# A mixture of experts: weight loads with a cast inside the DMA, against plain loads by one queue with the cast on VectorE

## The chip, the cores and the metric

The kernel runs on one core of a Trainium2 chip. The metric is the device time of one execution in microseconds (us); lower is better. The time before is 182.22 us, the median of three runs (182.13 to 182.71). The profiled execution spans 180.0 us from its first to its last instruction.

Engines are called PE (TensorE, matrix products), DVE (VectorE), ACT (ScalarE), POOL (GpSimd) and SP (SyncE). The last does no arithmetic here; it only issues transfers. All transfers, whoever issues them, run on the 16 DMA engines of the core.

## The reference

Eight experts, each with 256 tokens of 512 features, a first matrix 512 x 2048 and a second 2048 x 512. Everything is fp32 in memory.

```python
n_experts, capacity, hidden, expert_hidden = 8, 256, 512, 2048
# x [8, 256, 512]  w1 [8, 512, 2048]  w2 [8, 2048, 512]  b1 [8, 2048]  b2 [8, 512]
h = np.matmul(x, w1) + b1[:, np.newaxis, :]
h = np.maximum(h, 0)
return (np.matmul(h, w2) + b2[:, np.newaxis, :]).astype(np.float32)
```

Each w1[e] and each w2[e] has 4.194 MB in fp32, sixteen matrices in all; x and the result have 4.194 MB each.

## The kernel before

The products run in fp16. Every weight matrix is read by a transfer that GpSimd issues and that turns fp32 into fp16 on the way: the tile it writes is fp16. Three buffers hold w1, three hold w2. The last w2 has tiles of its own and comes in three pieces. x of the first two experts is loaded plain by SyncE and cast by VectorE, the rest by GpSimd with a cast.

```python
    LAG = 3
    w1_pool = ctx.enter_context(tc.tile_pool(name="w1", bufs=3))
    w2_pool = ctx.enter_context(tc.tile_pool(name="w2", bufs=3))
    w2t_pool = ctx.enter_context(tc.tile_pool(name="w2t", bufs=1))
    # ...
    def load_w1(e):
        w1_sb[e] = w1_pool.tile([P, nKC, M], fp16, tag="w1", name="w1sb")
        ordered(nc.gpsimd.dma_start(
            out=w1_sb[e], in_=w1[e].rearrange("(p kc) m -> p kc m", kc=nKC)
        ))
    # ... load_w2 and load_w2_piece alike
```

The first product needs x with its features in the partitions. VectorE makes this transposed xT from fp16 x in blocks of 32 x 32, in the middle of the first product of the expert before. The first product has 16 groups of four matmuls; ScalarE takes each group out of PSUM, adds b1 and applies the maximum with 0, and writes hT in fp16.

```python
                    nc.vector.transpose(out=out[:, tb, g], in_=block[:, tb])
    # ...
    def first_product(e):
        hT[e] = hT_pool.tile([P, nJ, T], fp16, tag="hT", name="hT")
        for j in range(nJ):
            bias_at = j * B + e * nB + nB - 1
            ph = psum_h.tile([P, T], fp32, tag="ph", name="ph")
            for kc in range(nKC):
                ordered(nc.tensor.matmul(
                    out=ph,
                    lhsT=w1_sb[e][:, kc, :].rearrange("p (q j) -> p q j", j=nJ)[:, :, j],
                    rhs=xT[e][:, kc, :],
                    start=(kc == 0),
                    stop=(kc == nKC - 1),
                ))
            nc.scalar.activation(
                out=hT[e][:, j, :],
                in_=ph,
                func=mybir.ActivationFunctionType.Relu,
                bias=b1T[:, bias_at : bias_at + 1],
                scale=1.0,
            )
            if j == nJ // 2 and e + 1 < E:
                transposes(e + 1)
```

The second product of expert e comes three steps after its first product (LAG), so four hT are held. It starts with the bias b2 as a matmul of one row and then runs 32 matmuls into two PSUM tiles, which VectorE and ScalarE copy to SBUF, one each. The stores of the first six experts are issued by GpSimd in the same queue as the loads, late, and the last two by SyncE and ScalarE.

```python
    for s in range(E + LAG):
        while ring and ring[0][0] <= s:      # loads and late stores, in a set order
            _, put, args = ring.pop(0)
            put(*args)
        if s < E:
            first_product(s)
        if s >= LAG:
            second_product(s - LAG)
```

Of the kernel before, what the change touches and what calls it, by code (L numbers as in the profile page):

```python
# [7 lines left out]


@with_exitstack  # L10
def kernel(
# [9 lines left out]
    nc = tc.nc  # L21
    fp32 = mybir.dt.float32
    fp16 = mybir.dt.float16
    E, T, H = x.shape
    M = w1.shape[2]
    P = 128
    nTB = T // P
    nKC = H // P
    nJ = M // P
    B = 32  # L30
    nB = P // B
    LAG = 3

    REUSED = {E - 2: 2, E - 1: 3}
    LATE = range(E - 2)


    PARTS = {E - 2: ((0, 25, False), (25, 121, True), (121, 128, False))}  # L40
    nXF32 = 2
    X_LOADS = {2: 2, 4: 4}

    def ordered(ins):
        return tc.keep_in_program_order(ins)

    singles = ctx.enter_context(tc.tile_pool(name="singles", bufs=1))
    w1_pool = ctx.enter_context(tc.tile_pool(name="w1", bufs=3))
    w2_pool = ctx.enter_context(tc.tile_pool(name="w2", bufs=3))
    w2t_pool = ctx.enter_context(tc.tile_pool(name="w2t", bufs=1))  # L50
    x_pool = ctx.enter_context(tc.tile_pool(name="xp", bufs=1))
    xT_pool = ctx.enter_context(tc.tile_pool(name="xTp", bufs=2))
    hT_pool = ctx.enter_context(tc.tile_pool(name="hT", bufs=LAG + 1))
    out_pool = ctx.enter_context(tc.tile_pool(name="outp", bufs=E - 2))
    psum_h = ctx.enter_context(tc.tile_pool(name="psum_h", bufs=3, space=bass.MemoryType.PSUM))
    psum_o = ctx.enter_context(tc.tile_pool(name="psum_o", bufs=2, space=bass.MemoryType.PSUM))

    ones1 = singles.tile([1, P], fp16)
    b2_sb = singles.tile([1, E * H], fp16)
    b1_rows = singles.tile([E * nB, M // nB], fp32)  # L60
    b1T = singles.tile([P, nJ * B + nB - 1], fp32)

    x16 = [None] * E
    xT = [None] * E
    w1_sb = [None] * E
    w2_sb = [None] * E
    hT = [None] * E
    results = []
    pending = {}

    def load_x(first, n):

        R = n * T // P
        t = x_pool.tile([P, R, H], fp16, tag=f"x{first}", name=f"x{first}")
        ordered(nc.gpsimd.dma_start(  # L75
            out=t, in_=x[first : first + n].rearrange("e (p r) h -> (e p) r h", r=R)
        ))
        for i in range(n):
            x16[first + i] = (t, i * (P // n), R)

    def load_w1(e):
        w1_sb[e] = w1_pool.tile([P, nKC, M], fp16, tag="w1", name="w1sb")
        ordered(nc.gpsimd.dma_start(  # L83
            out=w1_sb[e], in_=w1[e].rearrange("(p kc) m -> p kc m", kc=nKC)
        ))

    def load_w2(e):
        src = w2[e].rearrange("(p j) h -> p j h", j=nJ)
        w2_sb[e] = []
        t = w2_pool.tile([P, nJ, H], fp16, tag="w2", name="w2sb")  # L90
        ordered(nc.gpsimd.dma_start(out=t, in_=src))  # L91
        w2_sb[e].append((0, nJ, t))

    def load_w2_piece(e, lo, hi):
        t = w2t_pool.tile([P, hi - lo, H], fp16, tag=f"w2_{lo}", name=f"w2_{lo}")
        src = w2[e].rearrange("(p j) h -> p j h", j=nJ)
        ordered(nc.gpsimd.dma_start(out=t, in_=src[:, lo:hi, :]))  # L97
        if w2_sb[e] is None:
            w2_sb[e] = []
        w2_sb[e].append((lo, hi, t))  # L100

    def transposes(e):


        t, p0, R = x16[e]
        n = R // nTB
        xT[e] = xT_pool.tile([P, nKC, T], fp16, tag="xT", name="xT")
        for g in range(T // R // B):
            src = t[p0 + B * g : p0 + B * (g + 1)]
            for b in range(nB):  # L110
                block = src[:, :, b * (H // nB) : (b + 1) * (H // nB)].rearrange(
                    "p (n tb) (i kc) -> p tb kc n i", tb=nTB, kc=nKC)
                out = xT[e][b * B : (b + 1) * B].rearrange(
                    "p kc (tb g i n) -> p tb g kc n i", tb=nTB, i=B, n=n)
                if n == 1:
                    nc.vector.transpose(out=out[:, :, g, :, 0, :], in_=block[:, :, :, 0, :])  # L116
                    continue
                for tb in range(nTB):
                    nc.vector.transpose(out=out[:, tb, g], in_=block[:, tb])  # L119

    def first_product(e):
        hT[e] = hT_pool.tile([P, nJ, T], fp16, tag="hT", name="hT")
        for j in range(nJ):
            bias_at = j * B + e * nB + nB - 1
            ph = psum_h.tile([P, T], fp32, tag="ph", name="ph")
            for kc in range(nKC):
                ordered(nc.tensor.matmul(  # L127
                    out=ph,
                    lhsT=w1_sb[e][:, kc, :].rearrange("p (q j) -> p q j", j=nJ)[:, :, j],
                    rhs=xT[e][:, kc, :],  # L130
                    start=(kc == 0),
                    stop=(kc == nKC - 1),
                ))
            nc.scalar.activation(  # L134
                out=hT[e][:, j, :],
                in_=ph,
                func=mybir.ActivationFunctionType.Relu,
                bias=b1T[:, bias_at : bias_at + 1],
                scale=1.0,
            )  # L140
            if j == nJ // 2 and e + 1 < E:
                transposes(e + 1)

    def flush(e):
        dst, src = pending.pop(e)
        ordered(nc.gpsimd.dma_start(out=dst, in_=src))  # L146

    def store(e, po):
        if e in REUSED:
            out_sb = results[REUSED[e]]  # L150
        else:
            results.append(out_pool.tile([P, nTB, H], fp32, tag="out", name="out"))
            out_sb = results[e]
        nc.vector.tensor_copy(out=out_sb[:, 0, :], in_=po[0])  # L154
        nc.scalar.copy(out=out_sb[:, 1, :], in_=po[1])  # L155
        dst = out[e].rearrange("(p tb) h -> p tb h", tb=nTB)
        if e in LATE:
            pending[e] = (dst, out_sb)
            return
        for p0, p1, scalar in PARTS.get(e, ((0, P, False),)):  # L160
            (nc.scalar if scalar else nc.sync).dma_start(out=dst[p0:p1], in_=out_sb[p0:p1])

    def second_product(e):
        po = []
        for tb in range(nTB):
            t = psum_o.tile([P, H], fp32, tag=f"po{tb}", name=f"po{tb}")
            po.append(t)
            ordered(nc.tensor.matmul(  # L168
                out=t, lhsT=ones1, rhs=b2_sb[0:1, e * H : (e + 1) * H], start=True, stop=False,
            ))  # L170
        for lo, hi, t in w2_sb[e]:
            for tb in range(nTB):
                for j in range(lo, hi):
                    ordered(nc.tensor.matmul(  # L174
                        out=po[tb],
                        lhsT=hT[e][:, j, tb * P : (tb + 1) * P],
                        rhs=t[:, j - lo, :],
                        start=False,
                        stop=(j == nJ - 1),
                    ))  # L180
        store(e, po)

    x32 = []
    for e in range(nXF32):
        x32.append(out_pool.tile([P, nTB, H], fp32, tag="out", name="x32"))
        nc.sync.dma_start(out=x32[e], in_=x[e].rearrange("(p tb) h -> p tb h", tb=nTB))
    load_w1(0)
    ordered(nc.gpsimd.dma_start(  # L188
        out=b2_sb,
        in_=b2.rearrange("e h -> (e h)").rearrange("(o f) -> o f", o=1),  # L190
    ))
    ordered(nc.gpsimd.dma_start(out=b1_rows, in_=b1.rearrange("e (b i) -> (e b) i", b=nB)))  # L192
    nc.vector.memset(ones1, 1.0)  # L193

    for e in range(nXF32):
        t = x_pool.tile([P, nTB, H], fp16, tag=f"x{e}", name=f"x{e}")
        nc.vector.tensor_copy(out=t, in_=x32[e])  # L197
        x16[e] = (t, 0, nTB)
        if e == 0:
            transposes(e)  # L200


    for b in range(nB):
        nc.vector.transpose(  # L204
            out=b1T[b * B : (b + 1) * B, nB - 1 - b : nB - 1 - b + nJ * B],
            in_=b1_rows.rearrange("r (i j) -> r j i", j=nJ),
        )

    ring = []
    for s in range(1, E + LAG - 1):
        if s < E:
            if s in X_LOADS:
                ring.append((s - 2, load_x, (s, X_LOADS[s])))
            ring.append((s - 2, load_w1, (s,)))
        if s >= LAG:
            ring.append((s - 2, load_w2, (s - LAG,)))
    for lo, hi in ((0, 8), (8, 12), (12, 16)):
        ring.append((0, load_w2_piece, (E - 1, lo, hi)))  # L220
    for e in LATE:
        ring.append((e + LAG + 1, flush, (e,)))

    for s in range(E + LAG):
        while ring and ring[0][0] <= s:
            _, put, args = ring.pop(0)
            put(*args)
        if s < E:
            first_product(s)
        if s >= LAG:  # L230
            second_product(s - LAG)
    assert not ring and not pending


# [28 lines left out]
```

## Time and profile before

| | before |
|---|---|
| time, median of three runs | 182.22 us |
| span of the profile | 180.0 us |
| PE busy (matmuls) | 129.6 us, 72% |
| VectorE busy | 78.0 us, 43% |
| ScalarE busy | 62.2 us, 35% |
| read from HBM, written to HBM | 71.39 MB, 4.19 MB |
| bytes moved as written at the destination | 40.56 MB |
| longest waits on PE for w1 | 23.8 us in 6 waits, the longest 15.1 (the first) |

The profile counts a DMA by what it writes. A load that casts writes half of what it reads, so its GB/s in the slices must be doubled to be compared with a plain load's or a store's. The span is cut into 40 slices of 4.5 us; a digit is the busy share of an engine in tenths. A wait is put down to what ended it. A busy matmul is pipelined with its neighbours, so that the start of one to the start of the next is what it costs, not its own duration. A number in brackets such as (x35) counts the instructions in a stretch.

### The profile page before, as it was taken

How to read it: one execution, taken by the hardware profiler on the slowest of the kernel's cores; microseconds unless marked ns; L12 is line 12 of the kernel's file. 1: busy time of each engine (PE TensorE's matmuls, PEld its weight loads, DVE VectorE, ACT ScalarE, POOL GpSimd, SP SyncE). 2: the span in 40 equal slices, each digit the busy share in tenths (PEclk: the TensorE clock that was granted, in tenths of full speed). 3: DMA queues.
4: the chain of work that ended last, by engine and by line, in shares of the span. 5: the costliest groups of instructions: out<-in, count | busy, mean ns of one | idle time of the engine just before them, and what ended most of it. 6: DMA issues, size and time to landing. Idle time of an engine off the chain costs nothing.

```text
span 180.0 us, 1941 instructions
## 1 busy us (share of the span) xinstructions
PE 129.6 (72%) x784; PEld 86.2 (48%) x784; DVE 78.0 (43%) x111; ACT 62.2 (35%) x137; POOL 15.4 (9%) x32
## 2 busy tenths in 40 slices
PE   0006199969595960999979597959496977999960
PEld 0004179969592420795378245934195422434420
DVE  1999933986000199999980992001000100100030
ACT  0000559969592010483059003930196010010020
POOL 7000002020201010001010001000510101011000
PEclk9999999999998798589999889999999996999996
DMA  6998998999999999999999999999999999999996
GB/s 220 246 233 191 233 226 182 233 228 211 206 233 197 218 226 226 208 208 233 218 200 222 226 218 197 233 218 200 222 226 222 193 233 218 198 217 192 331 420 251
DMA packets 4404, 40.56 MB, mean 225 GB/s; under 512 B 524, under 2 KB 540, under 8 KB 2220
## 3 DMA queue, kind: packets, MB, share of 16 engines
q0 software_dynamic: 3808, 38.35, 96.6%
q1 hardware_dynamic: 476, 1.70, 2.5%
q10 hardware_dynamic: 112, 0.39, 0.6%
q8 instruction: 6, 0.10, 0.2%
q14 instruction: 2, 0.02, 0.0%
HBM read 71.39 MB, written 4.19 MB: 420 GB/s over the span
## 4 chain that ended last, share of the span: by engine, by line
DMA 80%; PE 13%; POOL 2%; issue 1%; another core or an unknown queue 1%; DVE 0%; POOLq 0%; DVEq 0%
DMA w1sb<-in_w_dram 44%; DMA w2sb<-in_w_dram 22%; DMA out_dram<-out 14%; PE ph L127 8%; PE po L174 5%; POOL w1sb L83 1%; DVE out L154 0%; PE po L168 0%; POOL b_rows L192 0%; POOL b_sb L188 0%; POOL x L75 0%; DVEq L154 0%; POOLq L146 0%; POOLq L247 0%
## 5 line engine op out<-in xcount | busy, mean ns | idle before, releaser
L127 PE MATMUL ph<-xT,w1sb 128*128 128x256 f16 x512 | 63.9, 290 | 33.9 <-DMA w1sb<-in_w_dram 23.8
L127 PEld LDWEIGHTS <-w1sb 128*128 128x128 f16 x512 | 59.2, 147 | 39.4 <-DMA w1sb<-in_w_dram 32.3
L119 DVE STREAM_TRANSPOSE xT<-x 32x256 f16<-32x256 f16 (+1 forms) x64 | 52.8, 886 | 30.3 <-DMA x<-in_x_dram 18.7
L134 ACT ACTIVATE hT<-ph,b1T 128x256 f16<-128x256 f32 x128 | 56.3, 474 | 20.2 <-PE ph L127 20.2
L174 PE MATMUL po<-w2sb,hT 128*128 128x512 f16 x224 | 54.5, 406 | 10.3 <-DMA w2sb<-in_w_dram 10.3
L174 PEld LDWEIGHTS <-hT 128*128 128x128 f16 x256 | 26.1, 103 | 45.7 <-issue 20.4
L154 DVE COPY out<-po 128x512 f32<-128x512 f32 x8 | 5.5, 692 | 62.5 <-PE po L174 44.1
L155 ACT COPY out<-po 128x512 f32<-128x512 f32 x8 | 4.7, 585 | 72.6 <-PE po L174 57.5
L116 DVE STREAM_TRANSPOSE xT<-x 32x256 f16<-32x256 f16 x32 | 14.0, 436 | 0.5
L83 POOL DMA_DIRECT2D w1sb<-in_w_dram x8 | 4.7, 591 | 63.0 <-PE ph L127 62.1
L91 POOL DMA_DIRECT2D w2sb<-in_w_dram x7 | 3.7, 534 | 54.5 <-PE po L174 54.5
L134 ACT ACT_TABLE_LOAD x1 | 1.3, 1283 | 20.1 <-DVE b1T L204 20.1
L174 PE MATMUL po<-w,hT 128*128 128x512 f16 x32 | 7.1, 379 | 0.0
L146 POOL DMA_DIRECT2D out_dram<-out x6 | 3.2, 539 | 32.0 <-DMA w2sb<-in_w_dram 27.5
L168 PE MATMUL po<-b_sb,ones 1*128 1x512 f16 x16 | 4.8, 379 | 0.0
L204 DVE STREAM_TRANSPOSE b1T<-b_rows 32x512 f32<-32x512 f32 x4 | 4.1, 1037 | 0.1
L197 DVE CAST x<-x 128x1024 f16<-128x1024 f32 x2 | 1.4, 694 | 3.0 <-DMA x<-in_x_dram 3.0
L168 PEld LDWEIGHTS <-ones 1*128 1x128 f16 x16 | 0.9, 92 | 2.1 <-issue 2.1
L97 POOL DMA_DIRECT2D w<-in_w_dram x3 | 1.6, 546 | 0.0
L75 POOL DMA_DIRECT2D x<-in_x_dram x2 | 1.1, 558 | 0.0
L192 POOL DMA_DIRECT2D b_rows<-in_b_dram x1 | 0.5, 525 | 0.0
L193 DVE MEMSET ones<- 1x128 f16 x1 | 0.2, 165 | 0.8 <-PEq L247 0.8
(5 smaller groups left out, 0.9 us busy)
## 6 DMA issues: line engine op xcount, KB each, us to landing
w1sb<-in_w_dram POOLq DMA_DIRECT2D x8, 2048.0 KB, 34.5
w2sb<-in_w_dram POOLq DMA_DIRECT2D x7, 2048.0 KB, 43.7
out_dram<-out POOLq DMA_DIRECT2D x6, 512.0 KB, 28.6
x<-in_x_dram SPq DMA_DIRECT2D x2, 512.0 KB, 3.6
x<-in_x_dram POOLq DMA_DIRECT2D x1, 1024.0 KB, 30.7
w<-in_w_dram POOLq DMA_DIRECT2D x1, 1024.0 KB, 35.7
w<-in_w_dram POOLq DMA_DIRECT2D x2, 512.0 KB, 38.8
x<-in_x_dram POOLq DMA_DIRECT2D x1, 512.0 KB, 24.1
```

What stands on the lines that cost most here:

```text
L83: ordered(nc.gpsimd.dma_start(out=w1_sb[e], in_=w1[e].rearrange("(p kc) m -> p kc m", kc=nKC)))
L91: ordered(nc.gpsimd.dma_start(out=t, in_=src))
L116: nc.vector.transpose(out=out[:, :, g, :, 0, :], in_=block[:, :, :, 0, :])
L119: nc.vector.transpose(out=out[:, tb, g], in_=block[:, tb])
L127: ordered(nc.tensor.matmul(out=ph, lhsT=w1_sb[e][:, kc, :].rearrange("p (q j) -> p q j", j=nJ)[:, :, j], rhs=xT[e][:, kc, :], start=(kc == 0),
L134: nc.scalar.activation(out=hT[e][:, j, :], in_=ph, func=mybir.ActivationFunctionType.Relu, bias=b1T[:, bias_at : bias_at + 1], scale=1.0,)
L146: ordered(nc.gpsimd.dma_start(out=dst, in_=src))
L154: nc.vector.tensor_copy(out=out_sb[:, 0, :], in_=po[0])
L155: nc.scalar.copy(out=out_sb[:, 1, :], in_=po[1])
L168: ordered(nc.tensor.matmul(out=t, lhsT=ones1, rhs=b2_sb[0:1, e * H : (e + 1) * H], start=True, stop=False,))
L174: ordered(nc.tensor.matmul(out=po[tb], lhsT=hT[e][:, j, tb * P : (tb + 1) * P], rhs=t[:, j - lo, :], start=False, stop=(j == nJ - 1),))
L204: nc.vector.transpose(out=b1T[b * B : (b + 1) * B, nB - 1 - b : nB - 1 - b + nJ * B], in_=b1_rows.rearrange("r (i j) -> r j i", j=nJ),)
```

## The change

The weights are no longer cast in the DMA. SyncE issues all large loads, plain fp32, in one queue and in the order in which they are needed, into a pool of two staging buffers of 32 KB per partition. VectorE casts from there into fp16 tiles, four instructions of 2048 columns to a matrix, and when a matrix has been cast, its staging buffer may be loaded again. One transfer brings x of the last six experts. GpSimd is left with the two biases and an identity matrix.

x is transposed by TensorE: eight transposes of 128 x 128 against the identity into one PSUM bank, then one copy by VectorE. They stand right behind the first product of the expert before. The second product now follows one step after the first (two hT buffers instead of four). All eight stores are issued last, by SyncE, in the queue of the loads. ScalarE makes all output copies but one. What is computed stays the same, and so do the shapes of both products. The aim is to take the work of the casting transfers off GpSimd and to keep one plain stream of large transfers, with nothing between the loads.

The core of the diff, with cuts marked by "...":

```diff
-    LAG = 3
+    nX0 = 2
...
-    w1_pool = ctx.enter_context(tc.tile_pool(name="w1", bufs=3))
-    w2_pool = ctx.enter_context(tc.tile_pool(name="w2", bufs=3))
-    w2t_pool = ctx.enter_context(tc.tile_pool(name="w2t", bufs=1))
-    x_pool = ctx.enter_context(tc.tile_pool(name="xp", bufs=1))
+    raw_pool = ctx.enter_context(tc.tile_pool(name="raw", bufs=2))
+    w_pool = ctx.enter_context(tc.tile_pool(name="w", bufs=3))
     xT_pool = ctx.enter_context(tc.tile_pool(name="xTp", bufs=2))
-    hT_pool = ctx.enter_context(tc.tile_pool(name="hT", bufs=LAG + 1))
-    out_pool = ctx.enter_context(tc.tile_pool(name="outp", bufs=E - 2))
+    hT_pool = ctx.enter_context(tc.tile_pool(name="hT", bufs=2))
+    out_pool = ctx.enter_context(tc.tile_pool(name="outp", bufs=E))
...
+    def load(key, pieces=None):
+        kind, e = key
+        if kind == "w1":
+            raw[key] = raw_pool.tile([P, nKC, M], fp32, tag="raw", name="raw1")
+            src = w1[e].rearrange("(p kc) m -> p kc m", kc=nKC)
... w2 and x alike
+        for lo, hi in pieces or ((0, src.shape[1]),):
+            o(nc.sync.dma_start(out=raw[key][:, lo:hi], in_=src[:, lo:hi]))
+
+    def cast(key, parts):
... dst is an fp16 tile of w_pool, or x_sb
+        for lo, hi in parts:
+            o(nc.vector.tensor_copy(out=dst[:, lo:hi], in_=t[:, lo:hi]))
...
     def transposes(e):
... the block transposes on VectorE go
+        for kc in range(nKC):
+            for tb in range(nTB):
+                o(nc.tensor.transpose(
+                    out=pt[:, kc, tb * P : (tb + 1) * P],
+                    in_=src[:, tb].rearrange("p (i kc) -> p kc i", kc=nKC)[:, kc],
+                    identity=ident,
+                ))
         xT[e] = xT_pool.tile([P, nKC, T], fp16, tag="xT", name="xT")
+        o(nc.vector.tensor_copy(out=xT[e], in_=pt))
...
+    loads = []
+    for s in range(E):
+        loads.append(("w1", s))
+        if s == nX0 - 1:
+            loads.append(("x", 0))
+        if s >= 1:
+            loads.append(("w2", s - 1))
+    loads.append(LAST)
...
+    AHEAD = 2
+    for key in loads[:AHEAD]:
+        load(key, PIECES.get(key))
+    for n, key in enumerate(loads):
+        kind, e = key
+        cast(key, ...)
+        if n + AHEAD < len(loads):
+            load(loads[n + AHEAD], PIECES.get(loads[n + AHEAD]))
+        if kind == "w1":
+            first_product(e)
+            if e + 1 < E and e + 1 != nX0:
+                transposes(e + 1)
+        elif kind == "x":
+            transposes(nX0)
+        elif kind == "w2":
+            second_product(e)
+    for e in range(E):
+        store(e)
```

## Prediction, made before the changed kernel was run

> **What bounds the kernel now.** I read the slices of the span first, then the DMA totals, then single stretches of time, and last the chain and the rows of single instructions.
>
> ```profile
> PE   0006199969595960999979597959496977999960
> DVE  1999933986000199999980992001000100100030
> DMA  6998998999999999999999999999999999999996
> HBM read 71.39 MB, written 4.19 MB: 420 GB/s over the span
> DMA 80%; PE 13%; POOL 2%; issue 1%; another core or an unknown queue 1%; DVE 0%; POOLq 0%; DVEq 0%
> ```
>
> The DMA row stands at 9 in nearly every slice, while PE and DVE have slices at 0: the DMA engines are never short of work, everything else sometimes is. The chain that ended last agrees (DMA 80%). The time is therefore bytes over rate. In the stretches the columns are: us, then busy time of PE, PEld, DVE, ACT, POOL, the granted clock, the DMA share, and GB/s as written at the destination.
>
> ```profile
> 3.00:4.00 1.00, 0.00 (x0) 0.00 (x0) 0.00 (x1) 0.00 (x0) 1.00 (x3) 1.00 1.01 406
> 40.00:60.00 20.00, 16.23 (x127) 13.73 (x125) 3.52 (x9) 13.33 (x31) 1.60 (x3) 0.94 1.02 216
> 100.00:140.00 40.00, 31.48 (x197) 20.95 (x197) 9.97 (x9) 15.10 (x34) 3.71 (x7) 0.96 1.01 216
> 170.00:175.00 5.00, 3.85 (x18) 1.57 (x16) 1.13 (x2) 1.01 (x2) 0.00 (x0) 1.00 1.02 419
> ```
>
> The casting loads write 216 GB/s of fp16, so they read 2 x 216 = 432 GB/s of fp32. The last stretch is nothing but fp32 stores: 419 GB/s at the same full share. The first is mostly the two plain fp32 loads of x: 406 GB/s. Counted in fp32 bytes, plain and casting transfers run nearly alike. A second reading of the load rate: on PE, products that wait for weights start at 91.36, 101.02, 110.73 and 120.46 us, so one weight matrix (4.194 MB) takes 9.7 us, or 432 GB/s.
>
> ```profile
> L127 PE MATMUL ph<-xT,w1sb 128*128 128x256 f16 x512 | 63.9, 290 | 33.9 <-DMA w1sb<-in_w_dram 23.8
> L119 DVE STREAM_TRANSPOSE xT<-x 32x256 f16<-32x256 f16 (+1 forms) x64 | 52.8, 886 | 30.3 <-DMA x<-in_x_dram 18.7
> L154 DVE COPY out<-po 128x512 f32<-128x512 f32 x8 | 5.5, 692 | 62.5 <-PE po L174 44.1
> L197 DVE CAST x<-x 128x1024 f16<-128x1024 f32 x2 | 1.4, 694 | 3.0 <-DMA x<-in_x_dram 3.0
> 91.36 7.20 PE ph L127 x64
> 101.02 8.77 PE po L174 x32
> ```
>
> These are the prices I need: a PSUM copy of 512 columns (692 ns), a cast of 1024 columns in SBUF (694 ns), a first product of 64 matmuls (7.20 us) and a second of 32 (8.77 us). The first product took 9.93 us at 72.19, after 6.13 us of idle, and the second takes 7.07 us when it is warm.
>
> **What the Trainium skill says.** *DMA: Bandwidth & Descriptors*, "Where 436 GB/s comes from", puts the ceiling of the 16 engines at 435 GB/s. This trace agrees: 432 GB/s, so no other way of issuing can gain more than 1%. The same page, "SWDGE vs HWDGE vs iDMA", says that a cast inside a DMA must be issued from GpSimd; that is why plain loads by SyncE need a cast on another engine. Its "Issuing engines are not separate DMA queues" says that all issuers share the same engines, so the move to SyncE by itself adds no bandwidth; the trace before has only 1.70 MB on such a queue and cannot test it. *VectorE: DVE Perf Modes*, "The perf-mode tier table", gives 1227 ns for an fp32 copy of 2048 elements; the trace's 694 ns for 1024 fits it (533 ns more for 1024 more).
>
> **The change part by part.**
>
> *Bytes.* Unchanged in HBM: 71.4 MB read and 4.2 MB written. Loads 71.4 / 0.432 = 165.3 us and stores 4.19 / 0.419 = 10.0 us, together 175.3. Ahead of them stand 1.7 us until data flows (SyncE issues at 0.74; the stretch 1 to 2 us has a DMA share of 0.30), and behind them about 1.5 us for the last store's completion (my choice). That floor is 178.5; the span before is 180.0. The old kernel has at most 1.5 us to give.
>
> *What VectorE loses and gains.* It loses 96 block transposes (52.8 + 14.0 = 66.8 us). It gains 64 weight casts of 2048 columns at 1.23 us (78.7 us), three such for x (3.7), and eight copies of 1024 columns from PSUM at 692 + 533 = 1.2 us (9.8). That is some 95 us in 190: VectorE does not become the bound by its sum. TensorE gains 64 transposes, some 1.0 us per expert (my choice, at about 0.13 us each, by the 0.11 us pitch of a first-product matmul, 7.20 / 64).
>
> *The new wait.* This is what costs. Before, a load had three fp16 buffers of its kind; now a load may be issued only when one of two fp32 buffers has been cast. From w2(0) on, w2 always takes one of them and w1 the other. VectorE works in order, and the copy of the next xT stands between the cast of w1(e) and that of w2(e-1); the copy waits for the transposes, and they stand behind first product e on PE. So from the landing T of w1(e) until the buffer of w2(e-1) is free: cast w1 4 x 1.23 = 4.9; first product 7.2; transposes 1.0; copy 1.2; cast w2 4.9; semaphores 0.2. Sum K = 19.4 us, or 22.1 with a cold first product (9.9). Then about 1.2 us from that until w2(e) flows (0.4 us of issue, the rest from the start of the span). The stream would want w2(e) after w2(e-1) and w1(e+1), at T + 2 x 9.7 - 0.5 = T + 18.9 (0.5 us: from the last byte to its semaphore, my choice). So the stream can dry out by B = 19.4 + 1.2 - 18.9 = 1.7 us warm, 4.4 cold. A gap ahead of w2(e) delays w1(e+1) as well and so gives the next round that much slack: two gaps in a row sum to about B. For w2(1) to w2(6), six gaps, that is 3 B: 5 to 13 us; I take 7, nearer to warm, as most first products in the trace are warm after gaps of 1 to 2.6 us.
>
> *The start.* w1(0) lands at 14.6 us (1.7, then 1.05 + 4.19 MB at 0.432, and 0.5 to the semaphore). w1(1) is cast 4.9 + 9.1 (a cold first product) + 1.0 + 1.2 + 4.9 + 0.2 = 21.3 us later, since its cast stands behind the copy of xT(1). Only then is w2(0) issued, flowing 22.5 us after T. The stream has only w1(1) and the rest of x (3.15 MB, 7.3 us) until then: 9.7 + 7.3 - 0.5 = 16.5. The gap is 6 us.
>
> *The end.* The stores, 10 us, now come after all loads and can't fill these gaps, as they are behind them in the same queue. On the other hand the last products run beside the first seven stores (8.7 us), so the computation's tail (three pieces of w2(7) landing, one cast, 8 matmuls) is mostly hidden.
>
> *Sum.* 178.5 + 6 + 7 = 191.5 us of span. The measured time before is 182.2 for a span of 180.0, so 2.2 more: 193.7, taken as 194.
>
> **The rivals.** (1) *Hidden anyway*: transposes and PSUM copy cost half of what I took and PE stays warm. Then K is 18.6, B under 1, and the gaps sum to 4 to 6 us: 186 to 188. For it: 7.2 us is the usual first product, and the idle before it is often near 2 us. Against it: the 6 us at the start hardly depend on it. (2) *Plain loads are slower*: at the 406 GB/s of the first fp32 loads the loads take 175.9 us, 10.6 more, but B falls to 20.6 - (2 x 10.3 - 0.5) = 0.5 and the start's gap to 5: about 178.5 + 10.6 + 5 + 2 + 2.2 = 198. For it: both plain measurements (406 and 419) lie under 432. Against it: the first microseconds of flow is a bad sample, with small transfers. (3) *Faster*: a purer stream, loads and stores apart, without casts in the DMA. It cannot pass the floor by more than the 1% between 432 and 435 GB/s: 178.5 - 1.4 + 2.2 = 179, and only with no gap at all. (4) *VectorE or PE becomes the bound*: PE cold throughout (9.9 + 8.8 + 1.0 = 19.7 us per expert) still meets 19.4 us of loads, so this comes out as (1)'s opposite: gaps of 18 us, 199.
>
> **Range and chances.** From rival 1's 187 to rival 4's and rival 2's 199 and a little: 187 to 201. Within 2% means up to 185.9, which needs nearly all gaps but the first to vanish: 0.10. Faster by 2% means 178.6, under the floor: 0.02.
>
> **What would show it.** In the profile after, the DMA row should have a hole at about 31 to 37 us and smaller ones every 20 or 40 us; SyncE's waits should name VectorE's casts for w2 loads and the long ones should fall there; full stretches of loads should show about 430 GB/s. VectorE's casts should last 1.23 us and its PSUM copies wait for PE. If full stretches show 400 to 410 instead, rival 2 holds. If there is no hole at 31 us, the chain of cast, product and copy is wrong. The prediction fails if TensorE's transposes are far dearer than 1 us per expert, if a cast slows while loads write SBUF, or if loads of one queue don't run at full rate back to back.

## The result, and the profile after

| | before | after |
|---|---|---|
| time, median | 182.25 us (182.13 to 182.71, 4 runs) | 201.67 us (200.57 to 202.71, 4 runs) |
| after / before | | 1.105 (95% interval 1.101 to 1.110) |
| span of the profile | 180.0 us | 199.7 us |
| last w2 cast from | | 188.6 us |

The change makes the kernel 10.5% slower. 194 us was predicted, with 187 to 201 as the range: the direction and the holes in the stream are as foreseen, the size is not.

The page of the changed kernel, busy tenths per slice of 5 us, then the bytes, the chain and four groups:

```profile
PE   0102892992986979896938978879459798999730
...
DVE  1827109605545049409071098136360396445310
...
DMA  8899895899999993999999968999999929999991
...
HBM read 71.39 MB, written 4.19 MB: 379 GB/s over the span
...
DMA 52%; DVE 25%; PE 15%; issue 2%; SPq 1%; ACT 0%; DVEq 0%
...
L110 PE MATMUL ph<-xT,w1sb 128*128 128x256 f16 x512 | 73.6, 307 | 32.0 <-DVE w1sb L88 32.0
...
L88 DVE CAST w1sb<-raw 128x2048 f16<-128x2048 f32 x32 | 37.0, 1221 | 21.6 <-DMA raw<-in_w_dram 21.6
...
L101 DVE COPY xT<-px 128x1024 f16<-128x1024 f16 x8 | 5.5, 692 | 61.1 <-PE px L95 61.1
L95 PE MATMUL px<-ident,x_sb 128*128 128x128 f16 x64 | 5.3, 230 | 4.7 <-DVE x_sb L183 4.7
```

The same bytes went at 379 GB/s instead of 420. The DMA row has digits of 2 to 6 at four places, where before it had none under 8 between its first and last slices. The chain has lost DMA share to VectorE and PE: transfers now wait for arithmetic. And the small copy of xT waits 61.1 us for PE, in the queue of the engine that must free the staging buffers.

Stretches of the changed kernel (us; busy time of PE, PEld, DVE, ACT, POOL; clock; DMA share; GB/s). All its transfers are plain, so no figure needs doubling:

```profile
32.75:35.75 3.00, 1.39 (x7) 0.91 (x7) 3.00 (x3) 0.46 (x1) 0.00 (x0) 0.71 0.00 0
75.75:78.75 3.00, 3.00 (x15) 1.36 (x14) 3.00 (x3) 0.00 (x0) 0.00 (x0) 1.00 0.00 0
118.75:120.75 2.00, 2.00 (x11) 0.91 (x10) 1.13 (x1) 0.00 (x0) 0.00 (x0) 1.00 0.00 0
161.00:164.00 3.00, 3.00 (x16) 1.35 (x15) 3.00 (x3) 0.00 (x0) 0.00 (x0) 1.00 0.00 0
36.00:75.50 39.50, 31.91 (x178) 21.39 (x177) 15.05 (x15) 15.27 (x33) 0.00 (x0) 0.77 0.97 415
121.00:160.00 39.00, 29.87 (x194) 21.12 (x192) 16.36 (x16) 16.60 (x36) 0.00 (x0) 0.91 0.99 422
183.00:186.50 3.50, 3.38 (x16) 1.56 (x16) 2.43 (x3) 0.00 (x0) 0.00 (x0) 1.00 0.96 298
195.50:198.25 2.75, 0.00 (x0) 0.00 (x0) 0.00 (x0) 0.00 (x0) 0.00 (x0) 0.50 0.07 27
```

Four stretches with no transfer at all, 11 us together, and VectorE casts in each. Even the flowing stretches, bounded by such holes, stay under 432. Near the end 3.5 us run at 298 GB/s, and a share of 0.07 for 2.75 us is about one of 16 engines (0.0625) still at work alone.

One round of the loop in the chain, with the start, duration and work of each piece:

```profile
38.19 19.52 DMA raw<-in_w_dram
...
62.49 9.60 PE ph L110 x61
72.09 0.46 PE px L95 x8
...
73.18 4.29 DVE w2sb L88 x4
```

w1(2) lands at 57.71, is cast, and then first product, transposes and copy stand ahead of the cast of w2(1), which ends at 77.8. SyncE issues the next w2 at once:

```profile
77.83 0.33 SPq L78 DMA_DIRECT2D raw<-in_w_dram  x1
```

Nothing had flowed since 75.75 or before, and the next bytes come at 78.75.

### The profile page after: what moved, and what is told of

It is laid out like the page before. It is cut to its first block, busy times and chain, and to the rows that moved or that the text cites. A ratio compares the mean times of both kernels' runs of the same rounds, so it can differ in the third digit from the quotient of the medians.

```text
span 199.7 us, 2051 instructions
## 1 busy us (share of the span) xinstructions
PE 142.4 (71%) x848; PEld 94.0 (47%) x848; DVE 88.9 (45%) x83; ACT 67.2 (34%) x144; POOL 1.9 (1%) x8
## 4 chain that ended last, share of the span: by engine, by line
DMA 52%; DVE 25%; PE 15%; issue 2%; SPq 1%; ACT 0%; DVEq 0%
DMA raw<-in_w_dram 52%; DVE w1sb L88 18%; PE ph L110 14%; DVE w2sb L88 5%; DVE x_sb L88 2%; PE po L138 1%; PE px L95 1%; SPq L174 0%; DVE xT L101 0%; SPq L78 0%; ACT out L150 0%; DVEq L88 0%
## 5 line engine op out<-in xcount | busy, mean ns | idle before, releaser
L110 PE MATMUL ph<-xT,w1sb 128*128 128x256 f16 x512 | 73.6, 307 | 32.0 <-DVE w1sb L88 32.0
L110 PEld LDWEIGHTS <-w1sb 128*128 128x128 f16 x512 | 62.7, 149 | 43.9 <-DVE w1sb L88 38.1
L138 PE MATMUL po<-w2sb,hT 128*128 128x512 f16 x256 | 60.9, 399 | 12.7 <-DVE w2sb L88 12.7
L88 DVE CAST w1sb<-raw 128x2048 f16<-128x2048 f32 x32 | 37.0, 1221 | 21.6 <-DMA raw<-in_w_dram 21.6
L88 DVE CAST w2sb<-raw 128x2048 f16<-128x2048 f32 x32 | 37.3, 1221 | 15.0 <-DMA raw<-in_w_dram 14.8
L150 ACT COPY out<-po 128x512 f32<-128x512 f32 x15 | 8.8, 587 | 72.5 <-PE po L138 72.5
L101 DVE COPY xT<-px 128x1024 f16<-128x1024 f16 x8 | 5.5, 692 | 61.1 <-PE px L95 61.1
L95 PE MATMUL px<-ident,x_sb 128*128 128x128 f16 x64 | 5.3, 230 | 4.7 <-DVE x_sb L183 4.7
L95 PEld LDWEIGHTS <-x_sb 128*128 128x128 f16 x64 | 4.7, 116 | 4.7 <-DVE x_sb L183 4.7
L148 DVE COPY out<-po 128x512 f32<-128x512 f32 x1 | 0.7, 692 | 1.1 <-PE po L138 1.1
## 6 DMA issues: line engine op xcount, KB each, us to landing
out_dram<-out SPq DMA_DIRECT2D x8, 512.0 KB, 19.4
rawx<-in_x_dram SPq DMA_DIRECT2D x1, 3072.0 KB, 12.7
```

What stands on the lines that cost most here:

```text
L88: o(nc.vector.tensor_copy(out=dst[:, lo:hi], in_=t[:, lo:hi]))
L95: o(nc.tensor.transpose(out=pt[:, kc, tb * P : (tb + 1) * P], in_=src[:, tb].rearrange("p (i kc) -> p kc i", kc=nKC)[:, kc], identity=ident,))
L101: o(nc.vector.tensor_copy(out=xT[e], in_=pt))
L110: o(nc.tensor.matmul(out=ph, lhsT=w[:, kc, :].rearrange("p (q j) -> p q j", j=nJ)[:, :, j], rhs=xT[e][:, kc, :], start=(kc == 0), stop=(kc ...
L138: o(nc.tensor.matmul(out=po[tb], lhsT=hT[e][:, j, tb * P : (tb + 1) * P], rhs=w[:, j, :], start=False, stop=(j == nJ - 1),))
L148: o(nc.vector.tensor_copy(out=results[e][:, tb, :], in_=po[tb]))
```

## The experiments

Theory A: a staging buffer is freed some 20 us after w1(e) lands, because the cast of w2(e-1) stands behind the copy of xT(e+1) and so behind first product e; two loads keep the queue filled for less than that, it runs dry, and each restart costs more than the 1.7 us of the prediction. Its rivals: plain loads, or SyncE's queue, are slow in themselves; or the transposes on PE, or the late stores, cost the time.

### e1_cast_first: the order on VectorE alone

```diff
         cast(key, ...)
         if n + AHEAD < len(loads):
             load(loads[n + AHEAD], ...)
+        while due:
+            transposes(due.pop())
         if kind == "w1":
             first_product(e)
             if e + 1 < E and e + 1 != nX0:
-                transposes(e + 1)
+                due.append(e + 1)
```

> The changed kernel with one change of order: VectorE casts w2(e-1) ahead of its copy of xT(e+1), so that the cast no longer waits for first product e. Theory A (the stream of loads runs dry because a staging buffer is freed only about 20 us after w1(e) lands, and each restart then costs some 3.5 us beyond its bytes; while it flows it runs at 431 GB/s): the buffer is free 14.4 us after the landing, no holes are left, the last w2 lands at about 170 us, span 179.5 to 182.5, time 181.5 to 184.5. Rival R (plain loads flow more slowly, 420 GB/s, holes or not): 186 to 188.5. Rival H (the holes have another cause than this order): about 200.

Measured 186.18 us, 1.020 of before (1.016 to 1.025). 15.5 of the 19.4 us are gone. The DMA row of its page, then the stretch that covers the stream (columns as above), then VectorE's queue in order of time:

```profile
DMA  6999999999999999999999999999999999999972
...
2.00:180.00 178.00, 137.25 (x843) 91.96 (x844) 88.28 (x81) 66.48 (x143) 0.91 (x3) 0.92 1.00 422
```

```profile
54.30 4.63 DVE L88 CAST w1sb<-raw 128x2048 f16<-128x2048 f32 x4 [5.14 <-DMA raw<-in_w_dram]
64.00 4.63 DVE L88 CAST w2sb<-raw 128x2048 f16<-128x2048 f32 x4 [5.07 <-DMA raw<-in_w_dram]
68.55 0.68 DVE L101 COPY xT<-px 128x1024 f16<-128x1024 f16 x1
```

Each cast of weights now waits for its landing and for nothing else: w1(2) lands at 54.20 us, w1(7) at 152.54, ten matrices in 98.3 us. The buffer of w2(1) is free 14.5 us after the landing of w1(2) (SyncE issues the next load at 68.66), and no digit of the DMA row shows a hole. So A is right on the order and the holes, and H falls. The time, however, misses A's range and lies at the low end of R's. One part of that is R's: the whole stream, its end included, runs at 422. The other is in the chain's end:

```profile
157.32 9.02 PE ph L110 x61
...
166.87 7.01 PE po L138 x32
...
174.42 7.03 PE po L138 x32
```

The last w2 piece is cast from 172.45 (A had its landing at about 170), but one first and two second products stand on PE behind the last w1 and end at 181.4; then the last copy and store.

### e2_stores_early: the stores alone, issued early

```diff
+        store(e)                       # right behind second_product's copies
     def store(e):
-        o(nc.sync.dma_start(
+        o(nc.scalar.dma_start(
...
-    for e in range(E):
-        store(e)
```

> The changed kernel with its stores issued by ScalarE as soon as each result is there, not last. Theory A: the holes stand where they did; a store falls into a stretch of flowing loads as often as into a hole, so the seven early stores save less than their 8.7 us, and the last store still waits for the last product: 196 to 200. Rival S (stores last are what the change lost, early ones fill the holes): about 191 to 193.

Its four runs spread from 197.94 to 205.23 us, and three of them fell in a slower state, so no ratio is given. The fastest, 197.94, lies in A's range, and all four are well above S's 191 to 193: the place of the stores is not what the change lost. That early stores save anything rests on this one run.

### e3_pe_transposes: the transposes alone, in the kernel before

```diff
-                    nc.vector.transpose(out=out[:, tb, g], in_=block[:, tb])
...
+                ordered(nc.tensor.transpose(out=pt[...], in_=src[...], identity=ident))
...
+        nc.vector.tensor_copy(out=xT[e], in_=pt)
```

They stand behind the whole first product, and x is loaded by rows to suit.

> The kernel before with one part of the change alone: x transposed by TensorE and copied by VectorE (692 ns each), instead of block transposes on VectorE. Theory A: the loads bound this kernel and a transposed expert costs PE 0.6 us, so the time stays within 1 us of 182.2. Rival T (the transposes on PE are part of the loss): 8 x 0.6 = 5 us more, 187.

Measured 182.62 us, ratio 0.9996 (0.998 to 1.001). The page of this kernel shows what was saved, to no effect:

```profile
DVE  1203700010100011001100110011000100100030
...
DMA  5998999999999999899989998999999999999994
```

VectorE is almost idle, its busy time down from 78.0 to 16.7 us, and the DMA row is as full as before. This holds where loads wait for nothing on PE or VectorE; in the changed kernel transposes and copy are part of the wait for the buffer, with 1.2 us a round, and e1_cast_first keeps both and wins the time back.

### e4_gpsimd_plain: the issuer

```diff
-            o(nc.sync.dma_start(out=raw[key][:, lo:hi], in_=src[:, lo:hi]))
+            o(nc.gpsimd.dma_start(out=raw[key][:, lo:hi], in_=src[:, lo:hi]))
```

> The kernel of e1_cast_first, with the same plain fp32 loads issued by GpSimd instead of SyncE. Theory A (all issuers share one stream of about 431 GB/s): within 2 us of e1_cast_first. Rival R in the form that SyncE's queue is the slower one: 4 us or more below e1_cast_first.

Measured 193.77 us, 1.059 (1.053 to 1.065): 7.6 more than e1_cast_first, which neither theory named. The stream itself is no different:

```profile
2.00:177.50 175.50, 131.32 (x812) 89.20 (x813) 85.97 (x80) 65.52 (x142) 13.18 (x23) 0.92 1.00 423
```

423 GB/s against 422, and from 60 to 150 us 424 in both. The edit had moved more than the issuer: with SyncE's queue rid of the loads, seven stores were issued as soon as they were ready and took turns with the loads. The last w2 piece is cast from 179.8 instead of 172.5 us. Seven stores are 3.67 MB, 8.7 us at 420 GB/s. So the issuer makes no difference to the rate. It also seems that in a stream without holes, stores behind the loads are a gain, as they fill the time that the last products need anyway; no run moves the stores alone in this kernel. In the changed kernel, which has holes to fill, the fastest run with early stores (e2_stores_early) was 3.7 us below it.

### e5_lag2 and e9_lag3: the products at the end

The part of the edit of e5_lag2 that sets the order of the loads:

```diff
...
-        if s >= 1:
-            loads.append(("w2", s - 1))
+        if s >= 2:
+            loads.append(("w2", s - 2))
+    loads.append(("w2", E - 2))
     loads.append(LAST)
```

> The kernel of e1_cast_first with w2(e-2) instead of w2(e-1) behind w1(e) in the queue and a third hT buffer, so that one first and three second products are spread over the last 29 us of loads, not one and two over the last 19. Theory A (what e1_cast_first still had over the DMA's own end is the products that stand on PE behind the last w1: loads and seven stores were done at 180.6 us, the last store's data came at 182.8): the products end before the last store's turn, span 182, time 183 to 184.5. Rival (the rest is the stream's own rate, 423 GB/s over all of e1_cast_first): no gain, 186.

Measured 184.96 us, 1.012 (1.010 to 1.014). The gain is 1.2 us of the 2 or 3 expected, and the time lies between A's range and its rival's 186. In its chain the last three second products follow one another without a gap to 178.3, so PE still ends last. The following two lines are the stretch from 60 to 150 us, of e5_lag2 and then of the kernel before:

```profile
60.00:150.00 90.00, 76.99 (x473) 50.48 (x471) 44.09 (x40) 35.57 (x77) 0.00 (x0) 0.93 1.00 428
```

```profile
60.00:150.00 90.00, 70.67 (x422) 45.56 (x421) 43.52 (x37) 31.06 (x69) 5.82 (x11) 0.94 1.02 217
```

Plain loads with no hole flow at 428 GB/s here, casting ones at 2 x 217 = 434. Over the same stretch e1_cast_first has 424 and e7_halves, below, 425. That is rival R's part: 1.4 to 2.3%. Why they differ at all stays open.

> The kernel of e5_lag2 with one step more: w2(e-3) behind w1(e), four hT buffers, and to make room seven output buffers with store 0 first. Theory A (what e5_lag2 still had over the end of its stream, 178.3 us, is the second products that stand on PE one behind the other to 178.3): the last product ends 3 us earlier, the last store follows the others without a gap, data ends at 179.5, span 181, time 182.5 to 183.5, so no better than the kernel before. Rival (a plain stream has a further loss in the end): 184 to 185.

Measured 184.51 us, 1.010 (1.007 to 1.014): within the noise of e5_lag2 and in its rival's range of 184 to 185, so the last products were not all that was left. It is the best form of the changed kernel and still not faster than the kernel before.

### e6_one_buffer: the cost of a restart by itself

```diff
-    raw_pool = ctx.enter_context(tc.tile_pool(name="raw", bufs=2))
+    raw_pool = ctx.enter_context(tc.tile_pool(name="raw", bufs=1))
...
-    AHEAD = 2
+    AHEAD = 1
```

> The kernel of e1_cast_first with one staging buffer: each of 16 loads is issued only when the load before it has been cast, so the stream is emptied 16 times, and the fixed cost F of an issue to its landing, beyond the bytes, is seen by itself. From the first landing at 16.3 us: casts 71 us, bytes 153 us, 16 F, then 10 us of stores and 1.7 us from span to time. Theory A (F = 3.5 us, as 34.79 to 48.0 us in the changed kernel for 9.7 us of bytes): 308. The prediction's step (F = 1.2 + 0.5 = 1.7): 280.

Measured 303.13 us, in one run. Less the 252 us that are not restarts in the expectation's sum (16.3 + 71 + 153 + 10 + 1.7), 51 us are left: 16 restarts cost 3.2 us each. Some of the 252 are estimates. Its issues show a restart directly (count, size, median us to landing):

```profile
raw<-in_w_dram SPq DMA_DIRECT2D x14, 4096.0 KB, 12.4
```

12.4 - 9.7 = 2.7 us, with nothing else in the queue. From the end of one cast to the start of the next, 13 rounds with a whole matrix take 12.1 to 13.6 us, 12.7 in the mean, which gives 3.0. So a restart costs about 3 us. The prediction's 1.7 is refuted, A's 3.5 is a little high.

### e7_halves: the buffers, with the order on VectorE kept

```diff
-    raw_pool = ctx.enter_context(tc.tile_pool(name="raw", bufs=2))
+    raw_pool = ctx.enter_context(tc.tile_pool(name="raw", bufs=4))   # half a matrix each
...
-        cast(key, ...)
-        if n + AHEAD < len(loads):
-            load(loads[n + AHEAD], ...)
+        for half in range(2):
+            cast(key, half)
+            if n + AHEAD < len(loads):
+                load(loads[n + AHEAD], half)
```

> The changed kernel, its order on VectorE kept, with four staging buffers of half a matrix in the place of two whole ones (the same bytes of SBUF): a half is loaded again as soon as its half has been cast, 2.3 us earlier. Theory A (each of the four holes is the buffer's release against the stream, B = K + F - 2L): each hole shrinks by 2.3 us, 9 us in all, less what more and smaller transfers cost: 191 to 195. Rival (the holes are set by something else, as the number of loads in flight): 199 to 202.

Measured 186.06 us, 1.011 (1.008 to 1.013), on the side of A but 5 us below its range. The expectation had the buffers come free only 2.3 us earlier. The trace has more (the last line is SyncE's, which issues the next half of a w2):

```profile
50.53 2.36 DVE L94 CAST w1sb<-raww 128x2048 f16<-128x2048 f32 x2 [1.68 <-DMA raww<-in_w_dram]
55.35 2.36 DVE L94 CAST w1sb<-raww 128x2048 f16<-128x2048 f32 x2 [2.46 <-DMA raww<-in_w_dram]
67.26 0.69 DVE L107 COPY xT<-px 128x1024 f16<-128x1024 f16 x1 [9.54 <-PE px L101]
67.87 4.62 DVE L94 CAST w2sb<-raww 128x2048 f16<-128x2048 f32 x4
...
70.25 4.87 SPq L79 DMA_DIRECT2D raww<-in_w_dram  x3
```

The first half of w1(2) is cast before the second lands, at 55.33, so half a cast less stands behind the landing as well. The first half of w2(1) is free 14.9 us after it, 5.2 us sooner than the 20.1 of the changed kernel and close to the 14.5 of e1_cast_first. Of the holes only half a microsecond at a third of the rate is left, at the first (32.5 to 33.0 us, 131 GB/s). This edit has four loads in flight instead of two, so alone it doesn't exclude its rival; e1_cast_first has two, as the changed kernel, and wins the same 15.5 us or so. What the two share is the earlier release.

### e8_after_again and e10_whole_last: the end

> The changed kernel once more, unaltered, for a second look at its holes and its end. Theory A: four holes at the same places within a few us, 200 to 203. In the first profile one engine's share of the DMA went on for 2.7 us after the others at the end; if it is a property of this kernel it is there again, if it is chance the end differs by as much.

Measured 202.41 us. The holes lie at the same places, and so does the end: one engine works on alone for 2 us and more after the others.

```diff
-    PIECES = {LAST: ((0, 8), (8, 12), (12, 16)), ("w2", E - 2): ((0, 8), (8, 16))}
+    PIECES = {}
```

> The changed kernel with its last two w2 loaded whole, not in two and three pieces. In both profiles of the changed kernel some 2 us of transfer are lost at 183 to 187 us, where the last pieces and the first stores meet, and one engine's share goes on 2 us behind the others at the end. If the pieces cause it, both are gone and the time falls by up to 4 us, less what the later landing of the first half costs (about 1 us): 198 to 200. If not: 201 to 204.

Measured 204.77 us, 1.123 (1.119 to 1.126): 3 us slower than the changed kernel. The loss is still there (261 GB/s from 183 to 187 us). The pieces aren't the cause; they help. What holds one engine back at the end stays open.

## Why the prediction was wrong in size

**Bytes, floor and issuer: right but for 1 to 2%.** The floor was taken at 432 GB/s; plain loads flow at 424 to 428. At 428 the loads cost 71.4 / 0.428 = 166.8 instead of 165.3 us, 1.5 more.

**VectorE's sums: right.** The weight casts take 1221 ns (1.23 predicted), and rival 4 fell: e1_cast_first has the same casts and products and took 186.18 us. Two of the small prices were too high: the copy of 1024 fp16 columns from PSUM takes 692 ns, not 1.2 us, and eight transposes 0.5 to 0.6 us, not 1.0.

**The new wait, K: right, its size partly by luck.** K is the time from the landing of w1(e) to the release of the buffer of w2(e-1). 57.71 to 77.83 is 20.1 us; with a warm product it was predicted as 19.4 and with a cold one as 22.1. First products show both: 6.9 to 9.8 us for the 61 matmuls behind the cast. At the later holes they were cold (9.6, 8.5 and 9.6 us), where warm ones had been assumed, and the rest of the chain was cheaper than assumed; the two errors nearly offset each other. e1_cast_first and e7_halves show that this wait makes the holes.

**The step that failed: "about 1.2 us from that until w2(e) flows" and "0.5 us: from the last byte to its semaphore".** Their sum, 1.7, was worked out from the start of a span and from a choice. e6_one_buffer has 3.2 by its whole time, 3.0 by its rounds. Of the 3.2, 1.0 or a little less lies from issue to data (34.79 to 35.75) and about 1.5 from last data to completion (w1(5)'s bytes end by 118.75, and it lands at 120.31; the last store's end at 198.25, the span at 199.7); the rest, some 0.7, I put down to the ramp, which no run isolates. *DMA: Bandwidth & Descriptors*, "Anatomy of one DMA — SWDGE (gpsimd) path", has a fixed cost of about 2.0 us for a transfer issued from GpSimd, most of it the write receipt; SyncE's transfers here show more; no run measures GpSimd's by itself. In the first gap, and in B for each of the three later ones, 1.5 us was missing: 6 us. With 3.2 in its place the prediction's own rule fits the trace. w1(2), w1(4) and w1(6) land at 57.71, 100.85 and 143.14 us, so four matrices took 43.1 and 42.3 us, 3.9 and 3.1 more than 4 x 9.8 (9.8 us is a matrix at 428 GB/s). K + 3.2 - 2 x 9.8 gives 3.7 and 2.7.

**The start: over-estimated.** From the landing of w1(0) to the issue of w2(0) it took 34.79 - 16.0 = 18.8 us, not 21.3: 2.5 us less, by a faster first product, copy and transposes. The first hole is where it was predicted. The later ones alternate as two gaps in a row should (at w2(2), w2(4) and w2(6)); for these K was 20.1, 19.1 and 20.1 us, 1.1 over three times 19.4, so 3 B comes to 5.1 + 1.1 = 6.2 us where 7 were taken: 0.8 less. The prediction's landing of w1(0) was added up wrongly (1.7 + 12.1 + 0.5 is 14.3, not 14.6; it was 16.0), which leaves its gap as it is.

**The end: missed.** The prediction let the stores flow at full rate and end with 1.5 us of completion. The completion took just that, but 3.5 us at 298 instead of about 420 GB/s lost 1.0 us, and one engine's 2.75 us came after the others. Together 3.7 us.

The sum, an estimate from these figures: 1.5 + 6.0 - 2.5 - 0.8 + 3.7 = 7.9 of the 8.2 us by which the span of 199.7 exceeds the predicted 191.5.

**The rivals.** Rival 1 (PE warm, cheap copies: 187) had the cheap copy and transposes right and the warm PE wrong, and the restart outweighed them (its K of 18.6 should be 19.4 - 1.1 = 18.3). Rival 2 (slower plain loads) holds for 1 to 2%. Rival 3 (faster) fell: no form of the changed kernel has a median under 184.5.

## What to carry to other kernels

With two staging buffers, write down the time from one landing to the release of the other buffer as a chain through every engine's queue, and compare it with two transfers less the cost of a restart, from issue to completion; what stands in front of the freeing instruction counts, not how busy its engine is (VectorE was busy 45%). Here the deadline was 2 x 9.7 - 3.2 = 16.2 us: releases after 19 to 20 us made holes, and releases after 14.5 and 14.9 us, by order or by halves, made almost none and won 15.5 of the 19.4 us back. Measure the restart instead of assuming it: here it was nearly twice the assumed one. Where a kernel runs at the rate of its bytes, a change that leaves the bytes as they are has little to win (here 1.5 us by the prediction's floor): look for that before its cost.

## What had not been expected of the hardware

A VectorE copy out of PSUM took 692 ns for 1024 fp16 columns and 692 ns for 512 fp32 columns: twice the elements in the same time. *VectorE: DVE Perf Modes*, "Why PSUM operands drop a tier", allows just that, up to 2x from PSUM but 1x for fp32; the prediction had priced the fp16 copy from fp32 figures. Four casts in a row took 4.63 us, 1.16 each, less than four times the 1221 ns of one.

The landing of a load isn't the moment its bytes stop flowing: some 1.5 us lie between. And in both profiles of the changed kernel one DMA engine ended 2 us and more after the others.
